# Two output projections of a hybrid decoder trunk: eight block products replaced by seven, in an order written out for four engines

## The chip, the cores and the metric

The kernel runs on one core of one Trainium2 chip. The metric is the device time of one execution in microseconds (us), the median of three runs. TensorE is called PE in the profile, VectorE DVE, ScalarE ACT, GpSimd POOL; SyncE (SP) issues the DMAs.

## What is computed

A trunk of two layers on x of 1 x 1024 tokens x 1024 channels, in float32. Each layer adds a token mixer and then a SwiGLU network to the residual stream h; a final norm closes the trunk.

```python
for layer in range(DEPTH):                     # DEPTH = 2
    hn = rms_norm(h, norm_mix_g[layer])
    h = h + (mixer_ab if layer % 2 == 0 else mixer_cd)(hn, ...)
    hn = rms_norm(h, norm_ffn_g[layer])
    h = h + (silu(hn @ w_gate[layer]) * (hn @ w_up[layer])) @ w_down[layer]
return rms_norm(h, norm_final_g)
```

Both mixers end in the same way: two mixers' outputs of 512 channels each are concatenated and multiplied by a 1024 x 1024 matrix.

```python
# mixer_ab: gated DeltaNet (o_a) and a gated short convolution (o_b)
return jnp.concatenate([o_a, o_b], axis=-1) @ w_out
# mixer_cd: HGRN2 (o_c) and dilated sliding-window attention (o_d)
return jnp.concatenate([o_c, o_d], axis=-1) @ w_out
```

The change concerns these two products `cat @ w_out`, the first norm behind them, and what stands at their two edges.

## The kernel before

**Layout.** Channels lie on the 128 partitions, tokens along the free axis: 8 blocks of 128 channels (`KT = 8`, `KH = 4`) by two halves of 512 tokens (`NH = 2`, `HT = 512`). A matmul takes a 128x128 piece of a weight as the stationary side and 128x512 of the activations as the moving side.

**Three matmuls for one.** Every float32 operand is split (`split`, lines 101 and 102) into a high part, a cast by ACT, and a low part, a subtraction by DVE that needs the cast. `mm3` (lines 125 to 127) then makes high x high, high x low and low x high, all into the same PSUM bank.

**Pools and rings.** `ring` holds the weights: raw ones as they land (`raw`, two buffers) and split ones (`w`, four units; `unit`). `hnp` holds eight "quarters" halves: a quarter is the high and low part of four channel blocks of one half (`quarter`). PSUM gives `psu` three banks, `psm` three and `psg` two. A tile that is asked for when its ring is full waits until the last use of the oldest. Pools that are closed give their memory to pools opened later.

**Mixers.** Layer 0 (`mixer_ab`, line 832) and layer 1 (`mixer_cd`) write their outputs block by block to DRAM scratch, `cat[layer][half]`. In layer 0 the last pieces are the DeltaNet chunks: the matmuls of line 1322, the product of line 1326 on DVE, the store of line 1327; in layer 1 the attention's last transposes (line 1782) and the stores of lines 1608 and 1785. In layer 0's front part, GpSimd computes a power that the normalised keys need (line 1049), and makes the memsets of lines 1157 to 1176; from the result DVE makes `nn` (line 1077), which TensorE transposes in line 1085. The matmuls of `short_conv` (weights by `wload`, gates in lines 983 to 1000) are mixed among them.

**Output projection** (`out_proj`, lines 810 to 829; a generator, called for each half from the loop behind the mixers at about line 1972). For one half it loads the eight channel blocks of `cat` (line 816, tile `cin`, in the mixers' pool `hp`) and splits each as it comes. Then, for the eight output blocks two at a time, it loads and splits the two weight blocks, makes 8 x 3 matmuls into one bank, adds the bank to h (line 824), squares the block for the norm (`tr.piece`, lines 179 to 186: squares on ACT, the running sum `acc` on GpSimd) and stores it (`tr.save`, line 216). `tr.begin` loads h of the half (line 166). The order of the engines' instructions is that of a scheduler of the framework here, which puts work of the first projection into the mixer's end: in the trace, half of the `cin` loads and casts stand among the mixer's last matmuls.

**The norm behind it.** `tr.rms(half)` sums over the partitions with eight 128x1 matmuls (line 198) and takes the power on GpSimd (line 203); `tr.spread` spreads the result by matmuls (line 212); `tr.scale` multiplies (line 222). In the second half's loop, rms(0) stands after its second block, and `norm_first` (lines 243 to 251) scales and splits the first half's two quarters b11 and b21 after the third.

**Behind it.** `mes.close()` closes the mixers' pool, `hx` is opened, and `Up.run` starts the network's up projection. Its first part, `turn` (line 583), is written in a fixed order for PE, DVE, ACT and POOL (`manual_schedule`: the order of the code is the order of the instructions on each engine). It loads and sums the first weights, splits three units (`part_a`), makes a first product `p1(0)`, then rms(1), and goes on. SP, which issues all these DMAs, is one queue in order: an issue that waits holds all behind it.

Of the kernel before, what the change touches and what calls it, by code (L numbers as in the profile page):

```python
# [54 lines left out]
def hybrid_trunk_kernel(ctx: ExitStack, tc: tile.TileContext, x_t, w_all, w_down, w_ba, vecs, c_f, c_i, c_rope, out):  # L55
# [186 lines left out]

    def norm_first(tr, row, dg):
        pb = tr.spread(dg)
        b11, b21 = quarter(), quarter()
        for i, q in enumerate((b11, b21)):
            for k in (0, 2):
                tr.scale(0, row, pb, range(i * KH + k, i * KH + k + 2))
                splits(q, tr.h[0][i], ((k, k + 2),))
        return b11, b21  # L250

    class Up:
# [330 lines left out]
        def turn(self, tr, row, b11, b21, hx, close, left, right):  # L583

            def sub(eng, dst, x, y):
                eng.tensor_tensor(dst, x, y, op=SUB)  # L586
# [6 lines left out]
            w2 = self.raw("g", 2, True)  # L593
            u0, g0 = (ring.tile([P, DM], F32, tag="raw", name="raw", bufs=2) for _ in range(2))
            dma(g0, w_all[W_AT["g", self.layer, 0]])
            dma(u0, w_all[W_AT["u", self.layer, 0]])
            V.tensor_tensor(sa[:, HT:], sa[:, :HT], sa[:, HT:], op=ADD)
            sub(V, sa[:, :HT], sa[:, HT:], ga[:, :HT])
            split(xu[:, 0, :], xu[:, 1, :], sa)
            self.named(1, xu, "s2", "s1")  # L600
            self.part_a(0, g0)
            self.part_a(1, ga)
            self.part_a(2, w2)
# [206 lines left out]
    def out_proj(name, cat_d, tr, src, order, half, hp):  # L810
        qs = {}
        for k in order:
            if k // KH not in qs:
                qs[k // KH] = quarter()
            f = hp.tile([P, HT], F32, tag="m", name="cin", bufs=4 - layer)
            dma(f, cat_d[k])
            split(hk(qs, 0, k), hk(qs, 1, k), f)
        tr.begin(half, src)
        for d0 in range(0, KT, 2):
            w = wload((name, d0), (name, d0 + 1))  # L820
            for i in range(2):
                o = proj(wk(w, i), qs, order, psg() if i else psu())
                h = tr.at(half, d0 + i)
                V.tensor_tensor(h, h, o, op=ADD)
                tr.piece(half, d0 + i)
                tr.save(half, d0 + i, hd[2 * layer][half])
                yield


    def mixer_ab(hn, rb, hp, tr, first, second, close):  # L830
# [46 lines left out]
        with ExitStack() as es:  # L877
# [87 lines left out]
            def short_conv(tick):  # L965
# [409 lines left out]
    def mixer_cd(hn, hp, second, close):  # L1375
# [6 lines left out]
        with ExitStack() as es:  # L1382
# [577 lines left out]
    for layer in range(2):  # L1960
# [133 lines left out]
```

## Time and profile before

| | |
|---|---|
| time, median of 3 runs (lowest to highest) | 2607.86 us (2607.75 to 2608.1) |
| the profiled execution's own time | 2610.04 us |
| its span | 2608.3 us |
| mean granted TensorE clock | 0.998 |
| layer 0: output projection, first to last matmul, about | 433 to 522 us |
| layer 1: output projection, about | 1871 to 1960 us |
| `cin` loads, and casts of them | 32 each |

How to read the lines that follow: a timeline row gives the start, the duration, the engine, the line of the kernel, the operation, the tile written `<-` the tiles read, the shape, how many such instructions the row groups, and in brackets the idle time before it on its engine with what ended it. Matmuls are pipelined: one row's duration is 0.39 us, but the next starts 0.23 us later, so counts go by starts. A row of windows gives, for a stretch, the busy time of PE, PE's weight loads, DVE, ACT and POOL with the number of instructions, then the granted clock, the DMA engines' share and GB/s.

### The profile page before, as it was taken

To read this page: it belongs to the slowest core of one execution; us is meant where nothing else is said; L and a number is where in the kernel's file an instruction comes from. 1 tells how busy PE (TensorE), PEld (TensorE's weight loads), DVE (VectorE), ACT (ScalarE), POOL (GpSimd) and SP (SyncE) were. 2 spreads that over 40 slices of the span, in tenths; PEclk is the share of its full clock that TensorE was granted. 3 is DMA by queue.
4 is the path that set the end of the run, shared out by engine and by line. 5 is a ranking of instruction groups with operands and counts; after the bars stand their busy time and mean duration, and the time that the engine had idled before them with its cause. 6 is when DMAs were issued, how large, how long until landed. Compare 5 with 4: busy or idle time off the path is not lost.

```text
span 2608.3 us, 37194 instructions
## 1 busy us (share of the span) xinstructions
PE 2588.8 (99%) x14307; PEld 2166.5 (83%) x14307; DVE 1654.8 (63%) x2784; ACT 1006.5 (39%) x1655; POOL 458.0 (18%) x434
## 2 busy tenths in 40 slices
PE   8999999999999999999999999999999999999998
PEld 6888888888888888888888888888888888888887
DVE  7877776575656665564665557478567665566553
ACT  4432123343333344333444335344444333334442
POOL 1111021334332300010000000000024433331001
PEclk9999999999999999999999999999999999999999
DMA  4434446424555688641212322224652445668853
GB/s 142 129 107 145 129 140 203 168 85 166 182 186 202 218 286 293 195 134 62 81 62 74 86 70 62 89 66 122 218 198 69 173 169 198 206 206 284 284 172 119
DMA packets 239699, 402.97 MB, mean 154 GB/s; under 512 B 30081, under 2 KB 114593, under 8 KB 239393
## 3 DMA queue, kind: packets, MB, share of 16 engines
q1 hardware_dynamic: 239520, 400.59, 46.4%
q8 instruction: 112, 1.84, 0.3%
q14 instruction: 67, 0.54, 0.1%
HBM read 280.36 MB, written 120.14 MB: 154 GB/s over the span
## 4 chain that ended last, share of the span: by engine, by line
PE 95%; DVE 3%; issue 1%; DMA 0%; ACT 0%; POOL 0%; SPq 0%; DVEq 0%; POOLq 0%; ACTq 0%
PE psu L125 20%; PE psu L127 19%; PE psu L126 19%; PE psg L125 5%; PE psg L127 5%; PE psg L126 5%; PE psm L125 4%; PE psm L127 4%; PE psm L126 4%; PE psm L1726 1%; PE psm L1700 1%; PE psg L1489 1%; PE psm L198 1%; PE psm L1715 1%; DVE h L586 1%
## 5 line engine op out<-in xcount | busy, mean ns | idle before, releaser
L125 PE MATMUL psu<-hnh,w 128*128 128x512 f32 x1328 | 530.4, 399 | 7.0 <-ACT w L101 7.0
L127 PE MATMUL psu<-hnh,w 128*128 128x512 f32 x1328 | 520.0, 392 | 0.0
L126 PE MATMUL psu<-hnl,w 128*128 128x512 f32 x1328 | 518.9, 391 | 0.9 <-DVE hnl L1885 0.8
L102 DVE TENSOR_TENSOR w<-raw,w 128x1024 fp32r<-128x1024 f32 (+1 forms) x314 | 375.6, 1197 | 152.3 <-ACT w L101 151.6
L101 ACT CAST w<-raw 128x1024 fp32r<-128x1024 f32 (+1 forms) x314 | 306.6, 977 | 298.9 <-PE psu L127 150.6
L125 PEld LDWEIGHTS psu<-hnh,w 128*128 128x128 f32 x1328 | 250.3, 188 | 57.2 <-ACT w L101 7.0
L127 PEld LDWEIGHTS psu<-hnh,w 128*128 128x128 f32 x1328 | 250.0, 188 | 54.0 <-DVE w L102 0.8
L126 PEld LDWEIGHTS psu<-hnl,w 128*128 128x128 f32 x1328 | 250.4, 189 | 51.1 <-DVE hnl L1885 1.3
L186 POOL TENSOR_TENSOR acc<-acc,sq 128x512 f32<-128x512 f32 x48 | 71.0, 1478 | 498.2 <-ACT sq L182 498.2
L102 DVE TENSOR_TENSOR hidq<-hr,hidq 128x1024 fp32r<-128x1024 f32 x72 | 82.3, 1144 | 74.7 <-ACT hidq L101 74.5
L296 POOL TENSOR_TENSOR ws<-raw 128x512 f32<-128x512 f32 x40 | 55.0, 1376 | 355.6 <-DMA raw<-in_dram 247.8
L125 PE MATMUL psu<-w,hnh 128*128 128x512 f32 (+1 forms) x320 | 113.1, 353 | 0.0
L102 DVE TENSOR_TENSOR w<-ws,w 128x1024 fp32r<-128x1024 f32 x38 | 50.7, 1334 | 97.0 <-ACT w L101 97.0
L127 PE MATMUL psu<-w,hnl 128*128 128x512 f32 (+1 forms) x320 | 111.2, 347 | 0.0
L126 PE MATMUL psu<-w,hnh 128*128 128x512 f32 (+1 forms) x320 | 111.1, 347 | 0.0
L101 ACT CAST hidq<-hr 128x1024 fp32r<-128x1024 f32 x72 | 70.4, 982 | 99.8 <-DMA hr<-ts 59.6
L125 PE MATMUL psm<-hidq,w 128*128 128x512 f32 (+1 forms) x275 | 106.0, 385 | 0.0
L126 PE MATMUL psm<-hidq,w 128*128 128x512 f32 (+1 forms) x275 | 105.8, 385 | 0.0
L127 PE MATMUL psm<-hidq,w 128*128 128x512 f32 (+1 forms) x275 | 105.8, 385 | 0.0
L1527 POOL COPY attn<-ac 32x128 f32<-32x128 f32 x32 | 13.3, 416 | 434.6 <-DVE ac L1493 381.6
L125 PE MATMUL psu<-hidq,w 128*128 128x512 f32 (+1 forms) x220 | 84.6, 385 | 0.0
L127 PE MATMUL psu<-hidq,w 128*128 128x512 f32 (+1 forms) x220 | 84.4, 384 | 0.0
(431 smaller groups left out, 5746.6 us busy)
## 6 DMA issues: line engine op xcount, KB each, us to landing
raw<-in_dram SPq DMA_DIRECT2D x228, 512.0 KB, 3.7
sd<-in_dram SPq DMA_DIRECT2D x44, 512.0 KB, 3.6
hid<-hid SPq DMA_DIRECT2D x88, 256.0 KB, 2.6
sd<-sd SPq DMA_DIRECT2D x44, 512.0 KB, 3.3
hr<-ts SPq DMA_DIRECT2D x40, 512.0 KB, 4.7
raw<-sd SPq DMA_DIRECT2D x40, 512.0 KB, 3.8
hd<-h SPq DMA_DIRECT2D x48, 256.0 KB, 4.3
h<-hd SPq DMA_DIRECT2D x48, 256.0 KB, 5.6
```

Source lines behind the costliest of these rows:

```text
L101: S.copy(hi, src)
L102: eng.tensor_tensor(lo, src, hi.bitcast(F32), op=SUB)
L125: T.matmul(o, lh, rh, start=first and i == 0, stop=False, **kw)
L126: T.matmul(o, lh, rl, start=False, stop=False, **kw)
L127: T.matmul(o, ll, rh, start=False, stop=last and i == n - 1, **kw)
L186: (eng or G).tensor_tensor(a, a, q, op=ADD)
L198: T.matmul(st[:, j:j + 1], x[:, j * P:(j + 1) * P], onesn, start=i + j == 0, stop=i == 1, skip_group_check=True)
L296: G.tensor_tensor(s[:, HT:], b[:, :HT], b[:, HT:], op=ADD)
L586: eng.tensor_tensor(dst, x, y, op=SUB)
L1489: T.matmul(od[r * 32:(r + 1) * 32, c * 32:(c + 1) * 32], a[:, z], x[:, z], start=True, stop=True, tile_position=(0, r * 32))
L1700: T.matmul(o[:, z], self.q[:, j * P:(j + 1) * P], self.k[:, (j - m + 1) * P:(j + 1) * P], start=True, stop=True)
L1715: T.transpose(o[:, i:i + P], s[:, i:i + P], ident)
```

## The change

The projection of both halves becomes one 2 x 2 block product of 512-blocks, with the blocks of `cat` (c11, c21 of half 0; c12, c22 of half 1) and of the weight, and is made with seven products in place of eight: four sums of the `cat` blocks (two by DVE, two by GpSimd) and four sums of the weight blocks. A product is 4 output blocks x 4 channel blocks x 3 matmuls. Some products add into banks that hold an earlier one, and a bank is added to h more than once.

- **Weights' sums.** `sums_out(layer, q)` loads two weight blocks into the `raw` ring, makes four sums of 128x512 on GpSimd in place, and stores them to DRAM scratch. Layer 0 calls it four times in `short_conv`, layer 1 four times in the third attention pattern's head loop.
- **Loads.** `fetch` loads four blocks of `cat` into one tile of the pool `hx`, which is now opened before the projection, after the mixers' pool is closed. `weights(m)` loads and splits the two units of product m, in two DMAs each.
- **Order.** Products 0 and 1 and their loads are placed by the scheduler; from then on PE, DVE, ACT and POOL follow the order of the code.
- **Norm and up.** rms(0) stands within product 5 (counted from 0), after a quarter of it; `normed` takes the place of `norm_first`. What `turn` did first is now `first_sums`, `first_loads` and `first_unit`, called within the projection.

```diff
+        def first_sums(self, hx):
             xa = hx.tile([P, 2, DM], F32, tag="hn", name="xa", bufs=6)
...
+        def first_unit(self, f):
+            self.part_a(f, (self.early[2][1], self.early[0][0][:, 0, :], self.early[1])[f])
...
-    def out_proj(name, cat_d, tr, src, order, half, hp):
...
+    def sums_out(layer, q):
+        a, b = (ring.tile([P, DM], F32, tag="raw", name="raw", bufs=2) for _ in range(2))
+        name = ("abo", "cdo")[layer]
+        dma(a, w_all[W_AT[name, q]])
+        dma(b, w_all[W_AT[name, q + KH]])
+        G.tensor_tensor(a[:, K1], a[:, K1], b[:, K1], op=SUB)
+        G.tensor_tensor(b[:, K1], b[:, K1], b[:, K2], op=ADD)
+        G.tensor_tensor(b[:, K2], b[:, K2], a[:, K1], op=SUB)
+        G.tensor_tensor(a[:, K2], a[:, K2], b[:, K2], op=SUB)
+        dma(sums_o[layer][q, :, 0, :], a)
+        dma(sums_o[layer][q, :, 1, :], b)
+
+    def out_proj(layer, tr, srcs, row, up, hx):
...
+        def fetch(half, k0):
+            t = hx.tile([P, KH, HT], F32, tag="hn", name="cat", bufs=6)
+            for i in range(KH):
+                dma(t[:, i, :], cat[layer][half][k0 + i])
+            return t
...
+        def weights(m):
+            for i in range(2):
+                raw = ring.tile([P, DM], F32, tag="raw", name="raw", bufs=2)
+                for j in range(2):
+                    dma(raw[:, j * HT:(j + 1) * HT], sources[m](2 * i + j))
+                u = unit()
+                split(u[:, 0, :], u[:, 1, :], raw)
+                ws[m, i] = u.rearrange("p z (j k c) -> p z j k c", j=2, k=KH)
+
+        def operand(src):
+            b = quarter()
+            splits(b, src)
+            return b
+
+        def product(m, o, b, first, qs=range(KH)):
+            for q in qs:
+                w = ws[m, q // 2]
+                mm3(o[q], [(w[:, 0, q % 2, k, :], w[:, 1, q % 2, k, :], b[0][:, k, :], b[1][:, k, :])
+                           for k in range(KH)], first, True, skip_group_check=True)
+
+        def add(half, d, o, n=None):
+            h = tr.at(half, d)
+            V.tensor_tensor(h, h, o, op=ADD)
+            if n is not None:
+                tr.piece(half, d, n=n)
+                tr.save(half, d, hd[2 * layer][half])
...
+        def normed(b, i, k, pb):
+            tr.scale(0, row, pb, range(i * KH + k, i * KH + k + 2))
+            splits(b, tr.h[0][i], ((k, k + 2),))
+
+        c11, c21 = fetch(0, KH), fetch(0, 0)
+        weights(0)
+        b11 = operand(c11)
+        weights(1)
+        b21 = operand(c21)
+        tr.begin(0, srcs[0])
+        x, z = [psu(), psm(), psm(), psm()], [psg(), psg(), psu(), psu()]
+        product(0, x, b11, True)
+        c12, c22 = fetch(1, KH), fetch(1, 0)
+        c = hx.tile([P, KH, HT], F32, tag="hn", name="cat", bufs=6)
+        weights(2)
+        comb(V, c, c22, c12, SUB, 2)
+        comb(V, c11, c, c11, ADD, 2)
+        t2 = operand(c11)
+        product(1, z, b21, True)
+        tr.begin(1, srcs[1])
+        E = mybir.EngineType
+        with tc.manual_schedule(engines={E.PE, E.DVE, E.Activation, E.Pool}):
+            t3 = operand(c)
+            for q in range(KH):
+                add(0, q, x[q])
+            weights(3)
+            comb(G, c21, c21, c11, SUB, 1)
+            comb(G, c12, c22, c11, SUB, 1)
+            product(2, x, t2, False)
+            for q in range(KH):
+                add(0, q, z[q], q)
+            t4 = operand(c21)
+            weights(4)
+            for q in range(KH):
+                add(1, q, x[q])
+            product(3, x, t3, False)
+            up.first_sums(hx)
+            t1 = operand(c12)
+            weights(5)
+            for q in range(KH):
+                add(1, q + KH, x[q])
+            product(4, x, t4, False)
+            b22 = operand(c22)
+            weights(6)
+            up.first_loads()
+            for q in range(KH):
+                add(0, q + KH, x[q], q + KH)
+            product(5, z, t1, True, (0,))
+            dg = tr.rms(0)
+            product(5, z, t1, True, (1,))
+            pb = tr.spread(dg)
+            product(5, z, t1, True, (2, 3))
+            add(1, KH, z[0], 0)
+            add(1, KH + 1, z[1], 1)
+            n11, n21 = quarter(), quarter()
+            normed(n11, 0, 0, pb)
+            add(1, KH + 2, z[2], 2)
+            normed(n11, 0, 2, pb)
+            up.first_unit(0)
+            add(1, KH + 3, z[3], 3)
+            normed(n21, 1, 0, pb)
+            normed(n21, 1, 2, pb)
+            up.first_unit(1)
+            product(6, z, b22, False)
+            for q in range(KH):
+                add(1, q, z[q], q + KH)
+                if q == 2:
+                    up.first_unit(2)
+        return n11, n21
...
@@ short_conv, layer 0
                         w = wload(("abg", 4 + h), ("abg", 8 + h))
+                        sums_out(0, h)
                         cs = fil.tile([P, 2 + T_LEN], F32, tag="cs", name="cs", bufs=1)
@@ attention heads, layer 1
                     q, k = swa_qk(h, p, tick)
+                    if p == 2:
+                        sums_out(1, h)
@@ behind the mixers
-        for half in range(NH):
-            steps = out_proj(("abo", "cdo")[layer], cat[layer][half], tr, residual[half],
-                             (4, 5, 6, 7, 0, 1, 2, 3), half, hp)
-            for d, _ in enumerate(steps):
-                if half == 1 and d == 1:
-                    dg = tr.rms(0)
-                if half == 1 and d == 2:
-                    b1 = norm_first(tr, row, dg)
         mes.close()
         hes = ExitStack()
         with ExitStack() as fes:
             hx = hes.enter_context(pool("hx"))
             up = Up(layer, fes.enter_context(pool("sums")))
+            b1 = out_proj(layer, tr, residual, row, up, hx)
```

More of the change, by code (lines that the diff above doesn't have):

```diff
@@ L241, in splits @@
             split(q[0][:, a:b, :], q[1][:, a:b, :], src[:, a:b, :], eng)
[L243 to L250, printed above, removed]
     class Up:
@@ L596, in turn, with sub @@
             dma(u0, w_all[W_AT["u", self.layer, 0]])
[L597 to L603, printed above, removed]
+            self.early.append((u0, g0))
+        def first_unit(self, f):
+            self.part_a(f, (self.early[2][1], self.early[0][0][:, 0, :], self.early[1])[f])
+        def turn(self, tr, row, b11, b21, hx, close, left, right):
+            def sub(eng, dst, x, y):
+                eng.tensor_tensor(dst, x, y, op=SUB)
+            (xa, xu), w2, (u0, g0) = self.early
+            ga, sa = xa[:, 0, :], xa[:, 1, :]
             s = self.sums(g0, u0)
@@ L807, in down @@
                     step(q)
-    def out_proj(name, cat_d, tr, src, order, half, hp):
[L811 to L820, printed above, removed]
-            for i in range(2):
[L822 to L827, printed above, removed]
+    K1, K2 = slice(HT, DM), slice(0, HT)
@@ new lines, in hybrid_trunk_kernel @@
+    sums_o = [dr.tile([KH, P, 2, DM], F32, name=f"so{i}") for i in range(2)]
+    def sums_out(layer, q):
[9 more added lines that the diff above has]
+        dma(sums_o[layer][q, :, 1, :], b)
```

20 lines of the change are left out of this document (17 added, 3 removed).

## The prediction

> **What bounds the kernel now.** I read the page's totals first, then its chain of work, then TensorE's waits, then narrow windows and timelines around the two output projections.
>
> ```profile
> span 2608.3 us, 37194 instructions
> PE 2588.8 (99%) x14307; PEld 2166.5 (83%) x14307; DVE 1654.8 (63%) x2784; ACT 1006.5 (39%) x1655; POOL 458.0 (18%) x434
> PE 95%; DVE 3%; issue 1%; DMA 0%; ACT 0%; POOL 0%; SPq 0%; DVEq 0%; POOLq 0%; ACTq 0%
> PE psu L125 <- ACT w L101: 7.0, 1, 7.0
> PE psm L198 <- ACT sq L182: 1.1, 1, 1.1
> 440.00:460.00 20.00, 20.00 (x90) 16.54 (x89) 10.66 (x12) 8.53 (x13) 5.03 (x4) 1.00 0.92 294
> 500.00:520.00 20.00, 20.00 (x90) 16.58 (x89) 14.61 (x14) 7.66 (x10) 10.82 (x7) 1.00 0.30 105
> ```
>
> TensorE is busy 99% of the span and holds 95% of the chain; its one long wait is the 7.0 us at the start. In layer 0's output projection (about 433 to 522 us; the two windows; their first column after the stretch is PE) it never stops. So a matmul taken away is time won, and every wait put before TensorE is time lost in full. The profiled execution took 2610.04 us (span 2608.3 and 1.74 around it), 2.2 above the median of 2607.86. I sum against 2610.04 and take the 2.2 off at the end.
>
> **The gain.** Before, a layer's projection is 2 halves x 8 column blocks x 8 k x 3 = 384 matmuls; after, 7 products x 4 x 4 x 3 = 336. So 96 go in two layers.
>
> ```profile
> 436.40 0.39 PE L125 MATMUL psg<-hnh,w 128*128 128x512 f32 x1
> 441.84 0.39 PE L125 MATMUL psu<-hnh,w 128*128 128x512 f32 x1
> ```
>
> These rows start two neighbouring groups of 24: (441.84 - 436.40)/24 = 0.2267 us each. Gain: 96 x 0.2267 = **-21.8 us**.
>
> **Edge of mixer and projection.** The new tiles (c11, c21 and so on, line 833 after) lie in a pool opened once the mixer's is closed. The written-out order of SP, one queue, has their loads behind the last store of `cat` and three loads of h (layer 0), and behind a weight load and one load of h (layer 1). Before, half of `cin` was loaded and split during the mixer.
>
> ```profile
> 431.77 1.13 PE L1322 MATMUL psm<-dgo,os 128*128 128x128 f32 x8
> 432.94 0.75 DVE L1326 SCALAR_TENSOR_TENSOR dgo<-psm,vec,szc 128x512 f32<-128x512 f32 x1 [0.18 <-PE psm L1322]
> 433.72 0.37 SPq L1327 DMA_DIRECT2D cat<-dgo  x1
> 434.18 4.23 SPq L166 DMA_DIRECT2D h<-in_dram  x8
> DMA to landing us min/median/max: 2.5/4.3/6.2
> 442.04 1.06 ACT L101 CAST w<-raw 128x1024 fp32r<-128x1024 f32 x1 [1.86 <-PE psg L127]
> 443.13 1.23 DVE L102 TENSOR_TENSOR w<-raw,w 128x1024 fp32r<-128x1024 f32 x1 [0.40 <-ACT w L101]
> 1869.99 0.60 PE L1782 MATMUL psu<-cf,ol 128*128 128x128 f32 x4
> 1872.24 1.23 DVE L102 TENSOR_TENSOR w<-raw,w 128x1024 fp32r<-128x1024 f32 x1 [0.73 <-ACT w L101]
> 1873.50 0.33 SPq L114 DMA_DIRECT2D raw<-in_dram  x1
> 1873.93 4.86 SPq L166 DMA_DIRECT2D h<-hd  x8
> ```
>
> Layer 0: the mixer's last matmuls end at 432.90. Three h issues at 4.23/8 = 0.53 put c11's first two loads at 435.8 and 436.2; the median landing of `cin`, 4.3 (the fifth row, from that tile's view), gives 440.5; the cast takes 1.06, so TensorE starts near 441.7, and its second matmul wants the low part (1.23 more). Loss about 9. The L1322 group waits on a chain through DVE and a landing, not on TensorE; 8 projection matmuls (1.8 us) that filled the time ahead of it have gone behind it: about 1.5 more. I take +10.5. Layer 1: the end is 1870.59, the raw load goes at 1873.50 after the split of 1872.24, one h issue (4.86/8 = 0.61), so c11 at 1874.5 and 1874.9, landed 1879.2, cast 1880.2: 9.6, less 0.3 that TensorE lost there anyway: +9.3. Together **+19.8**; with landings at 2.5 or 6.2 it is 16 to 24.
>
> **Product 2 (index from 0).** It reads t2 and adds into banks that DVE must first have emptied into h (`add(0,0,...)`), which the written order puts behind the t2 and t3 work: some nine 128x1024 passes. Its inputs c12 and c22 are the 22nd to 24th of 24 transfers of 256 KB; at the 294 GB/s of the first window 24 take 21.4 us, from 2.9 after the mixer's end. So 24.3 + 9 x 1.23 = 35.4 after the end, while TensorE is through products 0 and 1 at 9 + 96 x 0.2267 = 30.8. That is 4.6, of which the first passes, beside the last transfers, save some: **+3 a layer, +6** (0 to 12).
>
> **Products 3 and 4.** The code writes `weights(4)` ahead of the adds that empty the banks for product 3, and `weights(5)` ahead of those for product 4. The ring of split weights has four units, two to a product, so the second new unit waits for the running product's last matmul. Then TensorE's next product stands behind: cast, low part, add.
>
> ```profile
> 438.83 0.68 DVE L824 TENSOR_TENSOR h<-h,psu 128x512 f32<-128x512 f32 x1
> ```
>
> From product end to split end is 444.36 - 442.04 = 2.32 (ACT and DVE rows above), plus 0.68 = 3.0, plus 0.1 to 0.2 of handing on (0.18 in the 432.94 row): 3.15 each, two a layer, **+12.6**. The same split and add stand in the trace before, but beside 24 matmuls of the other bank, so they cost nothing there.
>
> **rms(0).** It stands after 12 matmuls (2.7 us) of product 5. From product 4's end: split 2.32, then the adds of h 4 to 7, each with a square and, for three, an accumulation on GpSimd, one behind the other.
>
> ```profile
> L186 POOL TENSOR_TENSOR acc<-acc,sq 128x512 f32<-128x512 f32 x48 | 71.0, 1478 | 498.2 <-ACT sq L182 498.2
> 443.00 0.62 ACT L182 ACTIVATE sq<-h 128x512 f32<-128x512 f32 x1
> ```
>
> 2.32 + 0.68 + 0.62 + 3 x 1.478 = 8.1; less 2.7: 5.4; I take 5.2 a layer, **+10.4** (4 to 6.3 each). Before, nothing waited here.
>
> **rms(1).** After product 4, DVE and ACT hold the whole norm of half 0 in strict order.
>
> ```profile
> 529.15 2.72 DVE L222 SCALAR_TENSOR_TENSOR h<-h,vec,psm 128x512 f32<-128x512 f32 x4 [2.47 <-PE psm L212]
> ```
>
> Two scalings (2 x 0.68), the cast 1.06 that DVE waits for, the low part 1.23: 3.65, four times, 14.6; plus four adds 2.7 and three splits of up's first units 3.7: 21.0. TensorE has 24 matmuls of product 5 and the 48 of product 6 in that time: 16.3. So product 6's adds end some 4 to 5 us late, and the squares and sums behind them meet an rms(1) where TensorE already waited 1.1 once before (the second row of waits above). **+5 a layer, +10** (2 to 7.5 each).
>
> **Mixers.** GpSimd gets four 128x512 operations per block row of the weights. In layer 0 the first four stand ahead of a memset and the power of L1049.
>
> ```profile
> raw<-in_dram SPq DMA_DIRECT2D x228, 512.0 KB, 3.7
> 232.90 1.23 DVE L102 TENSOR_TENSOR w<-raw,w 128x1024 fp32r<-128x1024 f32 x1 [0.25 <-ACT w L101]
> 231.39 0.96 POOL L1157 MEMSET suby<- 128x1024 f32 x1 [14.79 <-DVE cacc L1025]
> 239.46 1.64 POOL L1049 TENSOR_TENSOR r<-n,mhalf 128x8 f32<-128x8 f32 x1 [7.11 <-DVE n L1047]
> 513.63 2.27 POOL L296 TENSOR_TENSOR ws<-raw 128x512 f32<-128x512 f32 x1
> 243.95 0.18 DVE L1177 TENSOR_TENSOR s_c<-s_c,s_rk 128x32 f32<-128x32 f32 x1
> 246.63 0.60 PE L1085 MATMUL psm<-cf,nn 128*128 128x128 f32 x4
> ```
>
> The load for them goes out when the split of 232.90 frees its buffer, at 234.1, and lands 3.7 later; four operations at 1.27 (the row of 527.53 below) to 2.27 and the memset end between 244 and 248, so the power comes 4 to 9 us late. nn, done by 243.95 before, had 2.7 us to spare at 246.63: 1.5 to 6 us. I take **+3** in layer 0 and nothing in layer 1, where I see no such neighbour (0 to 3).
>
> **GpSimd beside VectorE.** The eight combinations on GpSimd per layer run while DVE is nearly full: 40 passes at 1.23 and 36 adds, scalings and sums at 0.68 make about 74 us of work in a stage of 336 x 0.2267 = 76 us of matmuls.
>
> ```profile
> 505.26 3.45 DVE L102 TENSOR_TENSOR w<-raw,w 128x1024 fp32r<-128x1024 f32 x2
> 506.21 1.41 POOL L186 TENSOR_TENSOR acc<-acc,sq 128x512 f32<-128x512 f32 x1 [0.83 <-ACT sq L182]
> 527.53 1.27 POOL L586 TENSOR_TENSOR ws<-xa 128x512 f32<-128x512 f32 x1
> 539.38 4.83 POOL L586 TENSOR_TENSOR raw<-xa,raw 128x512 f32<-128x512 f32 x1 [10.57 <-DMA raw<-in_dram]
> ```
>
> Two splits beside one GpSimd operation took 3.45 where two alone take 2.46; a GpSimd operation of 1.27 took 4.83 beside busy DVE. So of 8 x 1.27 = 10.2 us a layer DVE may lose between none and all. GpSimd loses more than DVE in these rows: I take 2 a layer, **+4** (0 to 20). [...]
>
> **TensorE's clock.** TensorE restarts slowly after a rest.
>
> ```profile
> 7.02 0.79 PE L125 MATMUL psu<-hnh,w 128*128 128x512 f32 x1 [7.02 <-ACT w L101]
> 10.98 0.39 PE L127 MATMUL psu<-hnh,w 128*128 128x512 f32 x1
> 20.97 0.39 PE L127 MATMUL psu<-hnh,w 128*128 128x512 f32 x1
> 23.33 0.49 PE L125 MATMUL psu<-hnh,w 128*128 128x512 f32 x1
> 24.00:28.00 4.00, 4.00 (x14) 3.19 (x13) 2.33 (x4) 0.00 (x0) 1.21 (x1) 0.57 0.45 175
> ```
>
> After 7.02 us idle eight matmuls took 3.96 us in place of 1.8 (2.1 lost); 2.4 us with one-column matmuls only (20.97 to 23.33) was followed by a granted clock of 0.57 for four (about 1.7 lost). So any of the six waits in a layer may cost 1.7 to 2.1 on top. Part is won back, as a slower product gives DVE time before the next wait. I take **+5** in all (0 to 22). [...]
>
> **Sum.** -21.8 + 19.8 + 6 + 12.6 + 10.4 + 10 + 3 + 4 + 5 = +49.0: 2610.04 + 49.0 = 2659.0, less 2.2: **2657**.
>
> **The rivals.**
> Only what follows from the written order costs anything (0.20): GpSimd, the mixers, the clock and product 2's start are free, rms(1) is 4 a layer: -21.8 + 19.8 + 12.6 + 10.4 + 8 = +29, 2637. For it: DVE idle in the windows before (10.66 of 20 busy). Against: DVE's load after.
> GpSimd shuts DVE out for every combination (0.14): 20 in place of 4: 2673. For it the row 3.45; against, 4.83.
> Every wait cools TensorE (0.10): six a layer, 12 x 1.7 = 20 in place of 5: 2672.
> The other side (0.05): c11's fetch leaves SP before the mixer's last store. Then DVE and ACT have the 9 us of lead that the edge costs, which also covers product 2 and rms(1); with the small terms at nothing, -21.8 + 12.6 + 10.4 = +1.2, with rms(0) at 4 -1.2: 2607 to 2609. It decides once c11 has been issued 9 us ahead of the last L1322 group, by about 423. Against it: memory that the mixer still holds, and one queue.
> My forecast has 0.51.
>
> **Range.** All terms low, 16 + 12.6 + 8 + 4 - 21.8 = +19: 2627. High: edge 24, product 2 12, 12.6, rms(0) 12.6, rms(1) 15, mixers 6, and half of GpSimd's and the clock's high ends (10 + 11) give +81; they will not all be high, as a wait lengthened early gives the next one lead: I stop at 2684, and begin at 2630. A measurement tells 0.2% (5.2 us). Faster 0.02, same 0.03, slower 0.95.
>
> **What would show it.** In the new trace: TensorE idle 8 to 11 us at both edges, released by ACT's cast of c11; 3 us ahead of products 3 and 4, released by a DVE add that starts right after a split; 4 to 6 us at the first L198 group, released by GpSimd; a wait at the second; L1049 starting after 242. Wrong would be: no idle at the edges, c11's loads ahead of the last `cat` store, or the adds ahead of the splits on DVE.

## The result and the profile after

The changed kernel takes 2693.8 us (median of 4 runs, 2692.05 to 2697.99), the kernel before 2607.98 beside it: ratio 1.0331, 95% interval [1.0313, 1.0349]. That is 85.8 us slower, where 49 were forecast; 2684 was the range's upper end.

From the page of the changed kernel: the span, the busy times, and the granted clock in 40 slices of 67 us.

```profile
span 2690.9 us, 37158 instructions
...
PE 2603.6 (97%) x14211; PEld 2173.1 (81%) x14211; DVE 1697.0 (63%) x2808; ACT 1009.3 (38%) x1647; POOL 519.2 (19%) x482
...
PEclk9999998889999999999999999999989999999999
```

TensorE has 96 matmul records fewer (14307 to 14211) and is busy 14.8 us longer. The clock row shows where: slices 7 to 9 lie in the first projection, slice 30 in the second.

TensorE's waits in the changed kernel (total us, times, longest):

```profile
PE psu L125 <- ACT hnh L101: 28.2, 4, 11.6
PE psm L198 <- POOL acc L186: 19.5, 4, 5.1
PE psu L125 <- DVE h L867: 13.4, 4, 3.5
PE psu L125 <- ACT w L101: 7.0, 1, 7.0
PE psg L1323 <- DMA yd<-scr_y: 2.7, 2, 1.5
PE psm L1204 <- DVE nn L1196: 2.3, 8, 0.9
```

The whole list comes to 80.3 us, against 12.7 before: 67.6 us of new idle time. In layer 0's projection it lies in six places (timeline of TensorE; the number in brackets is the wait):

```profile
452.93 0.80 PE L125 MATMUL psu<-hnh,w 128*128 128x512 f32 x1 [11.62 <-ACT hnh L101]
...
479.69 0.47 PE L125 MATMUL psu<-hnh,w 128*128 128x512 f32 x1 [2.90 <-DVE h L867]
...
495.92 0.47 PE L125 MATMUL psu<-hnh,w 128*128 128x512 f32 x1 [3.48 <-DVE h L867]
...
511.77 0.77 PE L125 MATMUL psu<-hnh,w 128*128 128x512 f32 x1 [3.08 <-ACT hnh L101]
...
533.56 1.86 PE L198 MATMUL psm<-onesn,acc 128*128 128x1 f32 x8 [5.13 <-POOL acc L186]
...
566.72 1.87 PE L198 MATMUL psm<-onesn,acc 128*128 128x1 f32 x8 [4.60 <-POOL acc L186]
```

In order: the edge, products 2, 3 and 4, rms(0), rms(1). Layer 1 has the same six: 10.39, 3.49, 3.50, 3.08, 5.14 and 4.62. The row of product 4 names a cast `hnh`, but the one that ends there is b22's, for product 6; product 4 reads t4, whose casts ended 21 us before, and waits for the add of its bank (shown below).

The other part is what follows each wait. Eight matmuls after the wait of 2.90 us:

```profile
480.24 0.63 PE L127 MATMUL psu<-hnh,w 128*128 128x512 f32 x1
480.67 0.63 PE L125 MATMUL psu<-hnh,w 128*128 128x512 f32 x1
...
483.23 0.58 PE L125 MATMUL psu<-hnh,w 128*128 128x512 f32 x1
483.64 0.40 PE L126 MATMUL psu<-hnl,w 128*128 128x512 f32 x1
```

Starts lie 0.43 us apart in place of 0.227, from 480.24 to 483.64: 1.6 us lost, after a wait of 2.9. Summed over the trace, matmuls in such stretches lose about 29 us (3.6 before, near the start), and the eight one-column groups of L198 in the projections, at 1.7 us from start to start in place of 0.9, another 7. So: -21.8 + 67.6 + 25 + 7 = +78, of the 82.6 us by which the span grew; the rest isn't broken down (the first interval after a restart is longer too: 0.31 us from the first start to the second behind product 2's wait, 0.56 behind product 4's).

### The profile page after: what moved, and what is told of

The parts are those of the page before. It is cut to its first block, busy times and chain, and to the rows that moved or that the text cites. A ratio compares the mean times of both kernels' runs of the same rounds, so it can differ in the third digit from the quotient of the medians.

```text
span 2690.9 us, 37158 instructions
## 1 busy us (share of the span) xinstructions
PE 2603.6 (97%) x14211; PEld 2173.1 (81%) x14211; DVE 1697.0 (63%) x2808; ACT 1009.3 (38%) x1647; POOL 519.2 (19%) x482
## 5 line engine op out<-in xcount | busy, mean ns | idle before, releaser
L125 PE MATMUL psu<-hnh,w 128*128 128x512 f32 x1280 | 518.3, 405 | 48.6 <-ACT hnh L101 28.2
L127 PE MATMUL psu<-hnh,w 128*128 128x512 f32 x1280 | 506.5, 396 | 0.0
L126 PE MATMUL psu<-hnl,w 128*128 128x512 f32 x1280 | 506.1, 395 | 0.1
L125 PEld LDWEIGHTS psu<-hnh,w 128*128 128x128 f32 x1280 | 244.6, 191 | 100.5 <-ACT hnh L101 29.4
L127 PEld LDWEIGHTS psu<-hnh,w 128*128 128x128 f32 x1280 | 244.3, 191 | 53.5 <-DVE w L102 0.8
L126 PEld LDWEIGHTS psu<-hnl,w 128*128 128x128 f32 x1280 | 244.7, 191 | 49.8 <-DVE hnl L102 1.5
L186 POOL TENSOR_TENSOR acc<-acc,sq 128x512 f32<-128x512 f32 x48 | 65.4, 1362 | 434.5 <-ACT sq L182 433.3
L125 PE MATMUL psm<-hnh,w 128*128 128x512 f32 x256 | 100.6, 393 | 0.0
L126 PE MATMUL psm<-hnl,w 128*128 128x512 f32 x256 | 99.9, 390 | 0.0
L127 PE MATMUL psm<-hnh,w 128*128 128x512 f32 x256 | 99.6, 389 | 0.0
```

The lines of the kernel that those rows point to most:

```text
L125: T.matmul(o, lh, rh, start=first and i == 0, stop=False, **kw)
L126: T.matmul(o, lh, rl, start=False, stop=False, **kw)
L127: T.matmul(o, ll, rh, start=False, stop=last and i == n - 1, **kw)
L186: (eng or G).tensor_tensor(a, a, q, op=ADD)
```

## The experiments

The theory after the result: the six waits are places in the written order, each ends where the prediction put it, and each also cools TensorE's clock. The rivals: VectorE is full (or is held up by GpSimd), so that a wait that is taken away comes back elsewhere; and the slow stretches come from something other than the waits. Each kernel is timed beside the kernel before on its chip; ratios are to it.

**e1: matmuls in four of the waits.** Their results, in a bank of z that the next product overwrites, are read by nobody.

```diff
+        warm(z[3], 0, 44)
         product(0, x, b11, True)
...
+            warm(z[3], 3, 12)
             product(3, x, t3, False)
...
+            warm(z[3], 4, 12)
             product(4, x, t4, False)
...
+            warm(z[3], 5, 20)
             dg = tr.rms(0)
```

> The changed kernel with matmuls whose results nobody reads put into four of TensorE's six waits per layer (44 ahead of product 0, 12 each ahead of products 3 and 4, 20 ahead of rms(0); fewer than fit into the waits). Theory (a wait cools TensorE's clock): the waits end when they did, and the 7 to 14 slow matmuls behind each of these four, 10.4 us in layer 0 and 9.6 us in layer 1 with the two slow groups of L198, run at 0.2267 us again: about 2674 us (2670 to 2679), granted clock above 0.98 by half of what is missing. [...]

Measured 2684.06 us, 1.0294 [1.0277, 1.0311]: 9.7 us gained, half of what was expected, and below all four executions of the changed kernel (2692.05 to 2697.99), where a cause other than the waits would have left it. 176 matmuls were added, and the kernel became faster. At rms(0) TensorE's timeline shows why:

```profile
524.55 4.69 PE L870 MATMUL psu<-w 128*128 128x512 f32 x20
529.92 1.05 PE L198 MATMUL psm<-onesn,acc 128*128 128x1 f32 x8 [0.68 <-POOL acc L186]
```

The L198 group at the same place of the work takes 1.05 us in place of 1.86. What is missing of the 20 us: product 2's wait grew (2.90 to 3.46 and 3.49 to 5.23; a faster product leaves VectorE less time), and slow stretches stayed behind short leftovers of waits, one of them of 1.94 us. Ahead of products 3 and 4, where the filled waits fell to 0.85 us and less, no slow stretch is left, and the mean granted clock rose from 0.981 to 0.990. The waits do cool the clock; filling them in part heals in part.

**e2: the adds ahead of the splits.** The same instructions in another order.

```diff
-            weights(4)
             for q in range(KH):
                 add(1, q, x[q])
+            weights(4)
             product(3, x, t3, False)
```

The same for the adds ahead of products 2 and 4 and for those of rms(0).

> The changed kernel with the adds that empty the banks written ahead of the splits behind them (products 2, 3, 4 and ahead of rms(0)); the same instructions. Theory (the written order makes the waits): no wait ahead of products 3 and 4 and next to none at the first rms(0), since three of four adds then run beside the product's own later quarters; 11.7 us of waits and some 8.5 us of slow clock a layer go, product 2's 3 us at most in part: 2650 to 2656 us. Rival (VectorE is full, or GpSimd keeps it from working, so that the waits move to the next place): above 2675.

Measured 2666.55 us, 1.0225 [1.021, 1.024]: 27 us gained, of some 40, a time between the two expectations. Gone are the waits ahead of product 4 and at rms(0); ahead of product 2, 0.68 and 1.91 us are left. The second rms's wait grew from 4.6 to 5.6 us in both layers. Product 3's grew too:

```profile
494.96 0.77 PE L125 MATMUL psu<-hnh,w 128*128 128x512 f32 x1 [5.88 <-DVE h L867]
```

Its adds still stood behind t4's split, which needs GpSimd's sum of c21.

**e5 and e6: two answers to that.** e5 puts those adds ahead of t4's split; e6 leaves them and gives the sums to VectorE.

```diff
# e5
+            for q in range(KH):
+                add(1, q, x[q])
             t4 = operand(c21)
-            for q in range(KH):
-                add(1, q, x[q])
# e6, beside e2
-            comb(G, c21, c21, c11, SUB, 1)
-            comb(G, c12, c22, c11, SUB, 1)
+            comb(V, c21, c21, c11, SUB, 2)
+            comb(V, c12, c22, c11, SUB, 2)
```

> The kernel e2_adds_first with the adds for product 3 also written ahead of t4's split (t4 needs GpSimd's sum of c21). In e2 product 3 still waited 5.9 and 4.4 us. Theory (those adds stood behind a split that waited for GpSimd): that wait and its slow clock (1.7 and 2.6 us) go: about 2652 us (2648 to 2657). Rival (GpSimd holds VectorE up wherever the split stands): the wait moves to product 4, above 2661.

> The kernel e2_adds_first with the two sums of cat by VectorE (four operations of 128x1024 per layer) in place of GpSimd (eight of 128x512). Theory (GpSimd's operations are slow beside a busy VectorE, and slow it in turn): product 3's wait falls under 1.5 us a layer: 2650 to 2657 us. Rival (VectorE has no 5 us to spare): the wait stays: above 2663.

e5: 2657.42 us, 1.0184 [1.0167, 1.0201]; product 3's wait is gone, and one of 2.94 and 1.79 us stands ahead of product 4: the theory for the most part, with some of the rival. e6: 2662.2 us, 1.0205 [1.019, 1.0221]; the wait stays (4.94 and 5.01 us), as the rival had it, since the sums now take 4.6 us of VectorE ahead of the same adds. What cures it is the adds' place in VectorE's order (e5), not the engine that makes the sums.

**e7: product 6's adds among the scalings of n21**, on top of e5.

```diff
-            normed(n21, 1, 0, pb)
-            normed(n21, 1, 2, pb)
-            up.first_unit(1)
             product(6, z, b22, False)
-            for q in range(KH):
-                add(1, q, z[q], q + KH)
-                if q == 2:
-                    up.first_unit(2)
+            add(1, 0, z[0], KH)
+            add(1, 1, z[1], KH + 1)
+            normed(n21, 1, 0, pb)
+            add(1, 2, z[2], KH + 2)
+            add(1, 3, z[3], KH + 3)
+            normed(n21, 1, 2, pb)
+            up.first_unit(1)
+            up.first_unit(2)
```

> The kernel e5_adds2 with product 6's adds put between the scalings of the second quarter, and two of up's three splits behind them. Theory (rms(1) waits since those adds stand behind the norm's strict order on VectorE): the waits of 5.6 and 0.5 us at the second rms and their slow clock (2.1 and 1.8 us) go in both layers: about 20 us under e5, near 2632 us. Rival (VectorE's backlog only moves, to p2(0)): under 8 us gained.

Measured 2640.26 us, 1.012 [1.0105, 1.0135]: 17.2 under e5, close to the 20 expected. In e5 the two waits of L198 on GpSimd came to 11.2 us (5.6 in each layer), in e7 to 0.9. So 10.3 us of idle time less made the kernel 17 us faster: the slow stretch and the two slow groups behind each wait went with it.

**e3: the edge.** b11 and b21 from the mixers' pool, as before the change; c11 and c21 are fetched again for the sums.

```diff
+        for k in (4, 5, 6, 7, 0, 1, 2, 3):
+            f = hp.tile([P, HT], F32, tag="m", name="cin", bufs=4 - layer)
+            dma(f, cat[layer][0][k])
+            split(hk(qs, 0, k), hk(qs, 1, k), f)
...
-        c11, c21 = fetch(0, KH), fetch(0, 0)
...
         c12, c22 = fetch(1, KH), fetch(1, 0)
+        c11, c21 = fetch(0, KH), fetch(0, 0)
```

> The changed kernel with the first half's operands b11 and b21 loaded and split from the mixers' pool as before the change (cin), and c11 and c21 fetched a second time for the sums, 16 loads of 256 KB more in all. Theory (the edge is a matter of where the loads of c11 stand): the waits of 11.6 and 10.4 us at the edges and 4.5 us of slow clock go. Two forms of it: if the loads of c12 and c22 come as early as TensorE now needs them, 2668 to 2673 us; if they stay bound to the end of the mixer by the queue and the memory, product 2's wait grows from 3 to about 12 us and the time is 2684 to 2692. Rival (the edge is bound by the last gated chunk, not by the loads): no change within 3 us.

Measured 2679.64 us, 1.0276 [1.0261, 1.0292]. No wait is left at the edges, and product 2 has it:

```profile
469.68 0.76 PE L125 MATMUL psu<-hnh,w 128*128 128x512 f32 x1 [12.07 <-DVE h L877]
```

That is the wait of the second form (11.68 us in layer 1): the 8 to 9 us of lead are spent in waiting for c12 and c22, which SP issues behind the mixer's last store and eight loads of h. The edge was the first of two waits for the same queue. The time lies under that form's 2684 to 2692 all the same (four executions, 2677.64 to 2684.1), and no run shows why.

**e4: layer 0's weight sums one iteration later.**

```diff
-                        sums_out(0, h)
+                        if h:
+                            sums_out(0, h - 1)
...
+                sums_out(0, 3)
```

> The changed kernel with layer 0's weight sums one iteration of the short convolution later, so that the first four stand behind the power of L1049 (before) on GpSimd. Theory (they delay the power, and the chain behind it waits twice more): the waits on nn, yd and yt in the first mixer, 6 us, and 3.3 us of slow clock go: 2683 to 2687 us. Rival (the two loads and two stores of each call hold up SP and the raw ring): 2691 to 2695.

Measured 2685.69 us, 1.0302 [1.0286, 1.0317], as the theory has it. The waits on nn beyond the 1.1 us that the kernel before has, and those on yd, are gone, and so are two of the mixer's slow stretches; 1.7 us on yt and 0.6 on dgo stay.

**e8: all of it**, with the sums of cat by VectorE, and the loads of h's first half behind those of c12, c22 and c11.

```diff
# beside e7 with the edits of e3 and e4
-        tr.begin(0, srcs[0])
         c12, c22 = fetch(1, KH), fetch(1, 0)
+        c11 = fetch(0, KH)
...
+        tr.begin(0, srcs[0])
+        c21 = fetch(0, 0)
...
-            comb(G, c21, c21, c11, SUB, 1)
-            comb(G, c12, c22, c11, SUB, 1)
+            comb(V, c21, c21, c11, SUB, 2)
+            comb(V, c12, c22, c11, SUB, 2)
```

> All edits together: e7, sums of cat by VectorE, layer 0's weight sums one iteration later, the first half's operands loaded from the mixers' pool, and h of half 0 loaded behind the cat blocks that product 2 needs. Theory (each wait has its own place in the written order, and the product's gain is real): edge, products 2 to 4, both rms and most of the first mixer's waits go; product 2 keeps 0 to 5 us a layer, since c12 and c22 need the mixer's last stores: 2588 to 2606 us, the first one under before. Rival (VectorE is full once TensorE no longer waits): above 2615.

Measured 2620.67 us, 1.0045 [1.003, 1.006]: the rival's number. But one wait holds most of the idle time that is left in the projections, ahead of product 3 in both layers (11.1 us in layer 1):

```profile
473.80 0.77 PE L125 MATMUL psu<-hnh,w 128*128 128x512 f32 x1 [8.70 <-DVE h L877]
```

Its adds stood behind the split of weights(3), and SP issued the loads for that one at 456.64, after all of h's second half and c21.

**e9 and e10: that place mended**, in e10 with the sums of cat by GpSimd as in the change.

```diff
             weights(3)
+            tr.begin(1, srcs[1])
+            c21 = fetch(0, 0)
             product(2, x, t2, False)
...
             for q in range(KH):
                 add(1, q, x[q])
+            comb(V, c21, c21, c11, SUB, 2)
+            comb(V, c12, c22, c11, SUB, 2)
             t4 = operand(c21)
```

> The kernel e8_all with the loads of weights(3) ahead of h's second half and of c21 on SP, and the sums of c21 and c12 behind the adds for product 3 on VectorE. In e8 product 3 still waited 8.7 and 11.1 us for adds that stood behind the split of weights(3), whose loads landed late. Theory (again a place in the two orders, not too little VectorE): that wait falls under 2 us, with 2.3 and 1.3 us of slow clock: 2597 to 2603 us, under before. Rival (VectorE is full): the wait moves to product 4 or 5: above 2610.

> The same with the two sums of cat by GpSimd, as in the change. Theory (GpSimd and VectorE slow each other by a few us, and the slow sums are now off TensorE's way until product 4): within 6 us above e9. Rival (the shared use is one of the large terms): more than 10 us above e9.

e9: 2611.35 us, 1.0011 [1.0002, 1.002]; e10: 2618.57 us, 1.0038 [1.0025, 1.005]. In e9 the wait moved to product 4, as the rival said:

```profile
481.70 0.77 PE L125 MATMUL psu<-hnh,w 128*128 128x512 f32 x1 [5.61 <-DVE h L877]
```

e10 is 7.2 us above e9, between the two expectations: GpSimd's sums cost a few us, as in e6 against e2 (4.3, measured on two chips).

**e11 and e12: the sum of c12, t1 and up's sums later**, behind the adds for product 4; in e12 those sums by GpSimd.

```diff
-            up.first_sums(hx)
-            t1 = operand(c12)
             for q in range(KH):
                 add(1, q + KH, x[q])
+            comb(V, c12, c22, c11, SUB, 2)
+            t1 = operand(c12)
             weights(5)
...
             weights(6)
+            up.first_sums(hx)
             up.first_loads()
```

> The kernel e9_order2 with the sum of c12 and t1 behind the adds for product 4, and up's first sums behind the split of weights(6). In e9 product 4 waited 5.6 and 6.4 us while VectorE worked 15.6 us without a pause between two groups of adds. Theory (that work was due later than where it stood): the wait falls under 1 us, with 2.3 and 4.2 us of slow clock: 2592 to 2600 us, under before for the first time. Rival (VectorE is full for the whole stage): it moves to product 5 or rms(0), above 2604.

> The same with the sum of c12 and up's two first sums by GpSimd. Theory (VectorE has just enough room once the order is right): within 5 us of e11, either way. Rival (VectorE is the bound): at least 5 us under e11.

e11: 2604.42 us, 0.9985 [0.9976, 0.9994], the only kernel here whose whole interval lies below 1, by 4 us, though 0.15% is less than the 0.2% that counted as a difference. It is still where the rival put it: the waits moved to the norm, and the time is above 2604. e12: 2607.23, 0.9995 [0.9986, 1.0004], within 5 us of e11, as its theory had it: work taken off VectorE and given to GpSimd gained nothing. No product waits in e11; what is left in the projections is 0.45 us at the second rms and this wait at rms(0), 1.81 us in both layers, with its slow stretch:

```profile
491.73 1.22 PE L198 MATMUL psm<-onesn,acc 128*128 128x1 f32 x8 [1.81 <-POOL acc L186]
492.81 1.84 PE L198 MATMUL psm<-onesn,sq 128*128 128x1 f32 x8
494.51 0.77 PE L125 MATMUL psg<-hnh,w 128*128 128x512 f32 x1
495.08 0.63 PE L126 MATMUL psg<-hnl,w 128*128 128x512 f32 x1
```

**e13, e14, e15: three ways to that last wait.** e13 asks for rms(0) a quarter of a product later; e14 does the adds for it earlier, ahead of b22's split; e15 is e14 with the splits of weights(6) and up's sums behind rms(0).

```diff
# e13, beside e11
-            product(5, z, t1, True, (0,))
+            product(5, z, t1, True, (0, 1))
             dg = tr.rms(0)
-            product(5, z, t1, True, (1,))
+            product(5, z, t1, True, (2,))
             pb = tr.spread(dg)
# e14, beside e11
-            b22 = operand(c22)
             for q in range(KH):
                 add(0, q + KH, x[q], q + KH)
+            b22 = operand(c22)
# e15, beside e14
-            weights(6)
-            up.first_sums(hx)
-            up.first_loads()
             product(5, z, t1, True, (0,))
             dg = tr.rms(0)
+            weights(6)
+            up.first_sums(hx)
+            up.first_loads()
```

> The kernel e11_order3 with rms(0) after two quarters of product 5 in place of one, and spread after three. In e11 the first rms still waited 1.8 us in each layer, and the granted clock fell behind it for 11 and 12 matmuls (2.3 and 2.6 us, and 0.6 us in the second L198 group). Theory (the wait itself cools the clock, so that a wait of 1.8 us costs 4.7): with no wait the slow stretch goes too: 9 to 10 us under e11, 2594 to 2597 us. Rival (the groups of one-column matmuls cool it, wait or not, as near the start of the kernel): only the waits go, 3.6 us: 2600 to 2602.

> The kernel e11_order3 with the adds, squares and sums for rms(0) ahead of b22's split (b22 is needed two products later); rms(0) stands after one quarter of product 5 as in e11. Theory (a wait and the slow stretch behind it go together, and the work for rms(0) was done too late, not asked for too early): the waits of 1.8 us at the first rms go with their slow stretches of 2.3 and 2.6 us, and nothing new is late, since rms(0) is where it was: 7 to 10 us under e11, 2594 to 2598 us. Rival (VectorE is the bound, and every wait that goes comes back at the next place, as in e13): within 3 us of e11.

> The kernel e14_b22_later with the splits of weights(6) and up's first sums behind rms(0) in the written order. In e14 TensorE waited 6.5 and 7.0 us for r: DVE's 0.15 us step between the norm's matmuls and GpSimd's power (v, line 201) stood behind 8 us of splits and sums. Theory (a place in the order): both waits and the slow matmuls behind them (0.7 and 2.1 us, and L212 at half speed) go: 2592 to 2600 us. Rival (VectorE is full, so that the splits now delay the scalings and product 6's adds): within 4 us of e11's 2604.

e13: 2606.26 us, 0.9991 [0.9982, 1.0]; e14: 2612.04, 1.0014 [1.0005, 1.0023]; e15: 2608.19, 0.9995 [0.9986, 1.0004]. None gains; e15 is where its rival put it, e13 and e14 fit neither of their expectations. Each took the wait at the first L198 away, and each met another one: e13 of 2.02 and 2.65 us at L212 and of 1.77 and 2.21 us at the second rms; e14 of 6.5 and 7.0 us at L212, since the 0.15 us step between the norm's matmuls and GpSimd's power stood behind 8 us of splits and sums on VectorE; e15, with that step in its place, of 4.0 and 3.9 us at the second rms. The e14 step on VectorE and what it let wait on TensorE:

```profile
497.44 0.15 DVE L201 TENSOR_SCALAR v<-psm 128x4 f32<-128x4 f32 x1
```

```profile
500.55 2.08 PE L212 MATMUL psm<-cf,r 128*128 128x128 f32 x8 [6.53 <-POOL r L203]
```

So from here on the rival holds in the main: in these orders, a wait that goes comes back at the next place. That no order could do better isn't shown. The same stretch of layer 0, by windows (PE, weight loads, DVE, ACT, POOL), in the kernel before and in e15:

```profile
455.00:500.00 45.00, 45.00 (x212) 37.67 (x211) 24.80 (x29) 16.12 (x20) 10.52 (x7) 1.00 0.61 203
500.00:540.00 40.00, 40.00 (x190) 33.53 (x189) 27.45 (x31) 13.98 (x18) 16.65 (x11) 1.00 0.23 74
```

```profile
455.00:500.00 45.00, 45.00 (x212) 37.57 (x212) 37.56 (x44) 21.33 (x25) 11.04 (x9) 1.00 0.67 240
500.00:540.00 40.00, 35.95 (x152) 29.61 (x151) 31.31 (x37) 16.23 (x20) 18.09 (x12) 0.87 0.19 68
```

VectorE works 68.9 of 85 us (37.56 + 31.31) where it worked 52.3 (24.80 + 27.45). Of the other 16, its timeline has 9.7 as five waits for TensorE's own results (three products, the norm's sums, the spread), 4.7 as four of 1.1 to 1.3 for ACT's cast of what VectorE has just made, a step that nothing overlaps in the strict order, and 1.8 for the cast of b22. As for the slow stretches: in e13 the first L198 groups had no wait ahead of them, and the matmuls behind them ran at full speed. But at e8's second rms, 0.47 us of wait and the same two groups were followed by half clock:

```profile
526.39:529.80 3.41, 3.14 (x22) 2.91 (x23) 1.16 (x2) 3.40 (x4) 1.13 (x2) 1.00 0.07 25
529.80:533.22 3.42, 3.42 (x11) 2.74 (x10) 3.42 (x4) 1.32 (x3) 1.02 (x1) 0.50 0.01 2
```

So in e11 the wait and the one-column matmuls together brought the stretch; that either would have done so alone isn't shown.

## Why the prediction was wrong

**The gain** was right as far as the rows go: 96 matmuls of 0.2267 us, and no run gives another cadence at full clock. No kernel here is without new waits, so none shows the 21.8 us in its total time.

**The six waits** were right, each in its place and near its price. Per layer, forecast against measured (layer 0, layer 1): edge 10.5 and 9.3 against 11.62 and 10.39; product 2 3 against 2.90 and 3.49; products 3 and 4 3.15 each against 3.48 and 3.08, 3.50 and 3.08; rms(0) 5.2 against 5.13 and 5.14; rms(1) 5 against 5.13 and 5.15 (two waits together). In sum 58.8 forecast, 62.1 measured. The chain of product 4 can be read off as it was added up, on ACT and on DVE; TensorE starts 0.15 us after the last row's end:

```profile
508.72 1.04 ACT L101 CAST w<-raw 128x1024 fp32r<-128x1024 f32 x1 [4.38 <-PE psm L127]
```

```profile
509.80 1.23 DVE L102 TENSOR_TENSOR w<-raw,w 128x1024 fp32r<-128x1024 f32 x1 [4.20 <-ACT w L101]
510.94 0.68 DVE L867 TENSOR_TENSOR h<-h,psu 128x512 f32<-128x512 f32 x1
```

e2, e5 and e7 then took most of these waits away by order alone, and e3 moved the edge's by an earlier load. Product 2's size was in part luck. In layer 0 VectorE began on its operands 21.7 us after the mixer's end (24.3 reckoned), TensorE was through product 1 after 35.5 (30.8), and the nine passes took 15.8 us (11.1). The last four of them ran beside GpSimd's sums. First the changed kernel, VectorE and GpSimd, then the same four splits in e6, where VectorE makes those sums later:

```profile
471.05 7.90 DVE L102 TENSOR_TENSOR hnl<-cat,hnh 128x1024 fp32r<-128x1024 f32 x4
471.25 12.35 POOL L875 TENSOR_TENSOR cat<-cat 128x512 f32<-128x512 f32 x6 [1.22 <-DMA raw<-so]
```

```profile
470.76 4.63 DVE L102 TENSOR_TENSOR hnl<-cat,hnh 128x1024 fp32r<-128x1024 f32 x4
```

The 3.3 us between them are as much as product 2's whole wait. And the row of 1.1 us that the text read as a wait at rms(1) before is one at the final norm, at 2599.21 us; in the projections before, no L198 group waited.

**TensorE's clock is the step that failed**: "I take +5 in all (0 to 22)". No run shows the 5; it measured 32: 25 in slow matmuls and 7 in slow L198 groups, after each of the six waits in layer 0 and five of the six in layer 1 (not after product 3's, at 3.50 us the longest of the products'; the last section shows why), and twice in the first mixer. With 32 in place of 5 the text's own sum comes to 2684, the end of its range; the six waits' 3.3 us more and the first mixer's 3.3 us of waits more carry it past. The rows for the price were there, 1.7 and 2.1 us a spell, and they held (1.6 to 2.9). Two reasons led away from them. The text reckoned that part would be won back, as a slow product gives DVE time before the next wait; but the waits of products 3 and 4 and of rms(0) begin at a product's end, however late it comes, and only product 2's and rms(1)'s can have that slack (product 2's grew by 0.6 and 1.7 us in e1, when the clock was mended in part; rms(1)'s by 1.0 in e2). And it counted a spell per wait in matmuls alone, where the norm's own groups stand in it too. The rival "every wait cools TensorE", given 0.10, was nearly the case (11 of 12), and even its 20 us were short.

**The mixers** were half right. The power of L1049 came 3 us late, by the four operations ahead of it (GpSimd, after):

```profile
236.23 1.28 POOL L820 TENSOR_TENSOR raw<-raw 128x512 f32<-128x512 f32 x1 [21.63 <-DMA raw<-in_dram]
...
240.33 1.29 POOL L823 TENSOR_TENSOR raw<-raw 128x512 f32<-128x512 f32 x1
241.56 0.95 POOL L1276 MEMSET suby<- 128x1024 f32 x1
242.47 1.65 POOL L1168 TENSOR_TENSOR r<-n,mhalf 128x8 f32<-128x8 f32 x1
```

nn then cost 1.2 us more than before, under the 1.5 to 6 of the forecast. But the text stopped there, and further waits come behind: on yd at 307 and 309 us (2.7), on yt at 377 (1.8), on dgo at 440 (0.6), with two slow stretches of 1.6 and 1.7 (which are within the clock's 25). That is 9.6 in place of 3. e4 took nn's and yd's share away by moving the sums; yt's and dgo's stayed, so the power's delay doesn't make them, and what does is not shown. Layer 1's mixer cost nothing, as taken.

**GpSimd beside VectorE**, +4 and at most 20, was of the right size: the sums by VectorE gained 4.3 (e6) and 7.2 us (e9 against e10). But in the changed kernel it isn't a term beside product 2's wait: the 3.3 us above lie within that wait.

**The other rivals.** "Only what follows from the written order" needed the clock, GpSimd and product 2 to be free, and none was. The other-side rival asked for a lead on the loads of c11. e3 gave it, and the lead went to product 2: c12 and c22 were behind the same queue. e8 to e11 show that much more than the loads' place is needed to come out even.

## What to carry to other kernels

In a kernel whose bound engine never stops, a wait costs its length and what the engine needs to come back to speed; here five of the six waits of about 3 us ahead of products 2 to 4 cost 4.6 to 6 us, and one only its own 3.5. Ask of each wait from where it is counted: one that begins at the bound engine's own last instruction isn't shortened by anything that happens earlier, and here order alone cured such waits (e2: 27 us for moving adds ahead of splits). And before work is taken from the bound engine, add up what the helpers must do in the shorter time: here VectorE went from 52 to 69 us in 85, and of the 21.8 us saved, 4 were left with the best order that was tried.

## What the runs showed of the hardware

- Whether a short wait slowed TensorE wasn't decided by its length alone in the changed kernel's trace, but by how much of it fell into one window of a grid. The granted clock changes 29 times there, always at a whole multiple of 3.4133 us from its other changes, within 0.003 us. The three changes in the kernel before lie at such multiples too, with the grid 1.6 us elsewhere, counted from the span's start. Product 3 in the changed kernel waits 3.48 us in layer 0 and 3.50 in layer 1. The first wait leaves 1.41 and 2.07 us idle in two windows (window less PE's busy time), the second 1.65 and 1.85, and only the first is followed by half clock:

```profile
490.44:493.85 3.41, 2.00 (x9) 1.31 (x7) 3.41 (x3) 2.03 (x3) 0.24 (x1) 1.00 0.06 20
493.85:497.27 3.42, 1.35 (x6) 1.16 (x7) 3.42 (x6) 0.00 (x0) 0.00 (x0) 1.00 0.56 165
497.27:500.68 3.41, 3.41 (x10) 2.64 (x9) 2.20 (x4) 1.75 (x2) 0.00 (x0) 0.50 0.39 142
```

```profile
1968.41:1971.82 3.41, 1.76 (x8) 1.13 (x6) 3.41 (x4) 1.81 (x2) 0.03 (x1) 1.00 0.05 18
1971.82:1975.24 3.42, 1.57 (x7) 1.34 (x8) 3.42 (x5) 0.00 (x0) 0.00 (x0) 1.00 0.59 193
1975.24:1978.65 3.41, 3.41 (x17) 2.81 (x16) 2.18 (x4) 1.97 (x3) 0.00 (x0) 1.00 0.34 119
```

  In the same trace, among the windows recorded at full clock that hold only 128x512 matmuls, every one with up to 1.85 us idle was followed by full clock, and each of the nine with 2.07 us or more by half clock, so that a wait needn't fill a window. The half-clock window behind product 2's wait (480.20 to 483.61) cost its matmuls 1.6 us.
- GpSimd's 128x512 sums took 16.6 us for eight in layer 0, beside the nearly full VectorE of the changed kernel, mostly 2.0 to 2.3 each, where such a sum took 1.28 in the mixer. VectorE was slowed too: four splits took 7.90 us there and 4.63 in e6.
- Matmuls that nobody needs made the kernel 9.7 us faster (e1): they fill time that was idle before, and the mean granted clock rose from 0.981 to 0.990.
